# Row-wise infinity norm: sending the bulk store after the last loads, and combining the tail rows one instruction later

## Chip, cores, metric

One core of a Trainium2 chip. The metric is the device time of one execution in microseconds (us), median of several.

## The reference

```python
x = np.random.randn(8192, 8192).astype(np.float32)       # 268 MB
return np.linalg.norm(x, ord=np.inf, axis=1)             # max |x| of each row: 8192 numbers, 32 KB
```

## The kernel before

Everything is read once and reduced on VectorE. 48 rows per partition are "bulk" (24 loads of 8 MB, two rows per partition each). The other 16 rows per partition are "tail": seven tiles in pieces that get smaller, then a last tile of 13 pieces, so that little work is left when the last byte lands. Bulk results go out in one store from the ACT queue, tail results in one from SP at the end. POOL waits for everything and clears the semaphores.

```python
    def absmax(o, i):
        nc.vector.reduce_max(out=o, in_=i, axis=X, apply_absolute_value=True)

    for a in range(A):                      # A = 6
        for n in range(G):                  # G = 4
            t = sbuf.tile([P, W + PAD], F32, tag="t")        # 3 buffers
            nc.sync.dma_start(out=t[:, :W], in_=x_b[a, n])
            absmax(r_bulk[:, a, n * B : (n + 1) * B], t[:, :W].rearrange(...))
    nc.scalar.dma_start(out=out_b, in_=r_bulk[:])            # 768 runs of 32 bytes

    for i, loads in enumerate(TAIL):        # 21 loads, 28 reductions into `part`
        ...
    # last tile
    for j, (b, w) in enumerate(LAST):       # 13 pieces, 2176 down to 640 columns
        final = left[b] == 0
        ...
        nc.sync.dma_start(out=t[:, to : to + w], in_=...)
        if final:
            absmax(r_tail[:, r : r + 1], t[:, to : slot[b] + parts_of[b]])
        else:
            absmax(t[:, k : k + 1], t[:, to : to + w])
        if j == 0:
            absmax(r_tail[:, : n_tail - B], part[:])         # combine the other tail rows
    nc.sync.dma_start(out=out_t, in_=r_tail[:])
```

All SP and ACT transfers share eight completion semaphores ("lanes") in rotation. A transfer is not issued before the previous user of its lane has landed.

## Time and profile before

| | kernel before |
|---|---|
| time, median (range) | 628.01 us (627.74 to 628.76), 3 runs; 627.96 over 6 |
| span in the profile | 626.4 us |
| load queue's share of the 16 DMA engines | 99.4% |
| VectorE busy | 552.9 us, 88% |
| bulk store, issue to landing | 59.1 us |
| SP's wait for the bulk store's lane | 24.3 us |

The loads fill the DMA engines from start to end, so the span is the time to read 268 MB plus a short end. Only what makes the loads end sooner, or shortens the path from the last landing to the end, can count. The lines that carry this are in the prediction.

### The profile page before, as it was taken

How to read it: one execution, taken by the hardware profiler on the slowest of the kernel's cores; microseconds unless marked ns; L12 is line 12 of the kernel's file. 1: busy time of each engine (PE TensorE's matmuls, PEld its weight loads, DVE VectorE, ACT ScalarE, POOL GpSimd, SP SyncE). 2: the span in 40 equal slices, each digit the busy share in tenths (PEclk: the TensorE clock that was granted, in tenths of full speed). 3: DMA queues.
4: the chain of work that ended last, by engine and by line, in shares of the span. 5: the costliest groups of instructions: out<-in, count | busy, mean ns of one | idle time of the engine just before them, and what ended most of it. 6: DMA issues, size and time to landing. Idle time of an engine off the chain costs nothing.

```text
span 626.4 us, 204 instructions
## 1 busy us (share of the span) xinstructions
DVE 552.9 (88%) x67; POOL 0.2 (0%) x4
## 2 busy tenths in 40 slices
DVE  0588988889988889888898888988889999999998
POOL 0000000000000000000000000000000000000000
DMA  9999999999999999999999999999999999999997
GB/s 402 469 402 452 418 452 418 448 423 402 469 402 469 402 469 402 469 402 469 402 469 402 465 406 452 418 452 418 452 404 426 438 428 425 439 423 431 426 422 311
DMA packets 9282, 268.49 MB, mean 429 GB/s; under 512 B 1856, under 2 KB 1856, under 8 KB 3392
## 3 DMA queue, kind: packets, MB, share of 16 engines
q1 hardware_dynamic: 8496, 268.45, 99.4%
q10 hardware_dynamic: 784, 0.02, 0.1%
q14 instruction: 2, 0.02, 0.0%
HBM read 268.44 MB, written 0.03 MB: 429 GB/s over the span
## 4 chain that ended last, share of the span: by engine, by line
DMA 63%; DVE 35%; issue 1%; another core or an unknown queue 0%; DVEq 0%
DMA t<-in_x_dram 63%; DVE r_bulk L140 24%; DVE part L140 8%; DVE t L140 3%; DVEq L220 0%; DVE r_tail L140 0%
## 5 line engine op out<-in xcount | busy, mean ns | idle before, releaser
L140 DVE TENSOR_REDUCE r_bulk<-t 128x2 f32<-128x16384 f32 x24 | 413.3, 17220 | 70.0 <-DMA t<-in_x_dram 70.0
L140 DVE TENSOR_REDUCE part<-t 128x1 f32<-128x8192 f32 (+20 forms) x28 | 121.6, 4410 | 0.9 <-DMA t<-in_x_dram 0.8
L140 DVE TENSOR_REDUCE t<-t 128x1 f32<-128x1664 f32 (+8 forms) x11 | 16.5, 1572 | 0.0
L140 DVE TENSOR_REDUCE r_tail<-t 128x1 f32<-128x644 f32 (+1 forms) x2 | 1.5, 814 | 0.0
L137 DVE MEMSET part<- 128x56 f32 x1 | 0.1, 105 | 0.9 <-PEq L209 0.9
L140 DVE TENSOR_REDUCE r_tail<-part 128x14 f32<-128x56 f32 x1 | 0.2, 211 | 0.0
L209 POOL MEMSET const-bfloat16-1.0<- 128x1 bf16 x1 | 0.1, 101 | 0.0
L209 POOL MEMSET const-uint8-127<- 128x1 uint8 x1 | 0.1, 101 | 0.0
L209 POOL MEMSET const-float32-0.0<- 128x1 f32 x1 | 0.1, 98 | 0.2 <-issue 0.2
L209 POOL MEMSET const-float32-1.0<- 128x1 f32 x1 | 0.1, 98 | 0.0
## 6 DMA issues: line engine op xcount, KB each, us to landing
t<-in_x_dram SPq DMA_DIRECT2D x2, 3392.0 KB, 37.3
t<-in_x_dram SPq DMA_DIRECT2D x1, 5376.0 KB, 40.6
t<-in_x_dram SPq DMA_DIRECT2D x1, 4864.0 KB, 32.9
t<-in_x_dram SPq DMA_DIRECT2D x1, 4800.0 KB, 33.0
t<-in_x_dram SPq DMA_DIRECT2D x1, 4672.0 KB, 34.9
t<-in_x_dram SPq DMA_DIRECT2D x3, 1536.0 KB, 28.7
t<-in_x_dram SPq DMA_DIRECT2D x1, 3520.0 KB, 42.9
t<-in_x_dram SPq DMA_DIRECT2D x1, 3328.0 KB, 40.4
```

The costliest lines, as they stand in the source:

```text
L137: nc.vector.memset(part[:], 0.0)
L140: nc.vector.reduce_max(out=o, in_=i, axis=X, apply_absolute_value=True)
L209: nc = _bacc.Bacc("TRN2", target_bir_lowering=False, num_devices=1)
```

## The change

Its intent: keep the small store out of the stream of loads, and let VectorE begin the last tile without waiting for the partials just written. `NoSync` is an order without a semaphore; `Sync` makes the ACT queue wait for VectorE.

```diff
     def absmax(o, i):
-        nc.vector.reduce_max(out=o, in_=i, axis=X, apply_absolute_value=True)
+        return nc.vector.reduce_max(...)
@@ after the bulk
-    nc.scalar.dma_start(out=out_b, in_=r_bulk[:])
@@ before the last tile
+    def after(ins, first, kind):
+        info = mybir.DependencyInfo(kind, mybir.DependencyReason.SCHED_ONLY)
+        tc.add_manual_dep(ins.ins, first.ins.name, info, reason="order")
@@ in the last tile
-            absmax(t[:, k : k + 1], t[:, to : to + w])
+            done = absmax(t[:, k : k + 1], t[:, to : to + w])
         if j == 0:
-            absmax(r_tail[:, : n_tail - B], part[:])
+            ins = absmax(r_tail[:, : n_tail - B], part[:])
+            after(ins, done, mybir.DependencyClass.NoSync)
+        if j == len(LAST) - 4:
+            ins = nc.scalar.dma_start(out=out_b, in_=r_bulk[:])
+            after(ins, done, mybir.DependencyClass.Sync)
```

More of the change, by code (lines that the diff above doesn't have):

```diff
@@ L139, in absmax @@
     def absmax(o, i):
-        nc.vector.reduce_max(out=o, in_=i, axis=X, apply_absolute_value=True)
+        return nc.vector.reduce_max(
+            out=o, in_=i, axis=X, apply_absolute_value=True
+        )
     for a in range(A):
```

## The prediction

> **What bounds the kernel now.** I read the page first, for which resource is full. These are its first line, the packet total, the queues and the two stores among the DMA issues (KB, then us from issue to landing):
>
> ```profile
> span 626.4 us, 204 instructions
> ...
> DMA packets 9282, 268.49 MB, mean 429 GB/s; under 512 B 1856, under 2 KB 1856, under 8 KB 3392
> ...
> q1 hardware_dynamic: 8496, 268.45, 99.4%
> q10 hardware_dynamic: 784, 0.02, 0.1%
> ...
> out_dram<-r_bulk ACTq DMA_DIRECT2D x1, 24.0 KB, 59.1
> out_dram<-r_tail SPq DMA_DIRECT2D x1, 8.0 KB, 1.4
> ```
>
> The load queue keeps the 16 DMA engines 99.4% busy: the kernel is a 268 MB read at 429 GB/s, with little at either end. The bulk store is 784 tiny packets (768 of 32 bytes and 16 for the semaphore) and takes 59.1 us to land, because it goes out in the middle of that read. So the second thing to read was who waited for it. First the load queue's own waits between 500 and 545 us, then the rates in four stretches (us, DVE busy, POOL busy, clock, DMA share, GB/s):
>
> ```profile
> SPq L158 <- DMA out_dram<-r_bulk: 24.3, 1, 24.3
> ```
>
> ```profile
> 41.20:486.40 445.20, 398.24 (x24) 0.00 (x0) 1.00 1.00 432
> 486.40:544.72 58.32, 57.86 (x10) 0.00 (x0) 1.00 1.00 430
> 544.72:578.44 33.72, 33.72 (x9) 0.00 (x0) 1.00 1.01 432
> ```
>
> ```profile
> 519.00:543.30 24.30, 23.84 (x4) 0.00 (x0) 1.00 1.01 435
> ```
>
> SP really stands for 24.3 us, because the store sits in the rotation of eight completion semaphores and a load needs its lane. But in just those 24.3 us the DMA engines run at a share of 1.01 and 435 GB/s: two loads issued before were still draining. The wait is in the queue, not in the data. What the store does show is the second line: 430 GB/s while its packets are in the stream, against 432 before and after.
>
> Third, the end: the chain of waits, last pieces (start, us, what), and the order of time around 606 us:
>
> ```profile
> 588.91 0.02 issue
> 588.93 17.66 DVE part L140 x7
> 606.59 0.02 issue
> 606.61 0.21 DVE r_tail L140
> 606.82 16.01 DVE t L140 x11
> ```
>
> ```profile
> 604.17 2.41 DVE L140 TENSOR_REDUCE part<-t 128x1 f32<-128x2176 f32 x1
> 606.48 2.76 SPq L179 DMA_DIRECT2D t<-in_x_dram  x2
> 606.61 0.21 DVE L140 TENSOR_REDUCE r_tail<-part 128x14 f32<-128x56 f32 x1
> 606.74 2.41 DVE L140 TENSOR_REDUCE t<-t 128x1 f32<-128x2176 f32 x1
> ```
>
> From 599.1 us VectorE never idles. The first piece of the last tile has landed at 606.46 (SP, which waits for that same semaphore, goes on at 606.48), yet its reduction starts at 606.74. By the trace's semaphore records the pieces land 0.16 to 0.38 us before their reductions start, all the way to the last one (landed 623.61, started 623.86). So the end is set by VectorE running just behind the loads: a fixed amount taken off VectorE after 599.1, or all loads landing earlier, shows in full; either can only move until the other holds it.
>
> **What the Trainium skill says.** "DMA: Bandwidth & Descriptors", section "Queues, rings and completion order", says each DMA engine goes round its queues by packet. The trace agrees: 784/16 = 49 store packets per engine were let in one or two at a time between load packets, first at 487.84, last at 542.95 us. Its section "Issuing engines are not separate DMA queues" says that ACT and SP share the 16 engines; so the store takes time from the loads wherever it overlaps them, as the dip to 430 GB/s shows. "VectorE: DVE Perf Modes", section "The DRAIN you can't avoid", says an instruction that reads what the one just before wrote needs a semaphore, and that one instruction between them removes the hazard. The trace agrees on the cost side: VectorE reductions otherwise start some 80 ns before their predecessor's recorded end (604.168 + 2.410 = 606.578 would allow 606.50), but the one that reads the partials, written just before, started at 606.613, 35 ns after that end. "Perfetto Trace Analysis", section "DMA Instruction — HWDGE (DVE, Sync)", says a write's semaphore follows only after the write is confirmed, slow above all to HBM. The tail store agrees: issued at 624.705, packets from 625.546 to 625.749, landed at 626.131.
>
> **The change part by part.** (1) The store leaves the stream of loads. Each of its 784 packets takes 9 ns in the DMA records: 784 x 9 / 16 = 0.44 us per engine. A second way: the six loads that land between 486.40 and 544.72 bring 49,152 columns, 1.1865 ns each; the bulk loads run at 19.33 us / 16,384 = 1.180. 49,152 x 0.0065 = 0.32 us. I take 0.35 us by which every later load lands earlier. VectorE can follow: the two gaps where it waited for a load (0.46 us before 536.40, 0.36 us before 584.17) mean that it had finished early there and starts with the data.
> (2) SP's 24.3 us wait goes, and the store leaves the lane rotation; the loads behind it are queued about 24 us earlier. Nothing drains faster: 0.
> (3) The reduction of the partials moves behind the first piece of the last tile. It no longer reads what was just written, so piece one can start at 606.50 instead of 606.74, the partials' reduction runs after it, and the second piece starts at 606.50 + 2.326 + 0.128 = 608.95 instead of 609.07: 0.117 us saved (2.326 and 0.128 are the distances from start to start before). The built program shows one new instruction: piece one now has two waits, so a separate semaphore wait stands before it (21 ns where the trace has such). It may not get in until the load has landed at 606.46, so I count 0.08 us. The loads allow it: the smallest lead of a landing over its reduction is 0.16 us.
> (4) The store now goes out when VectorE has finished the tenth of 13 pieces, before at 621.277 + 1.076 = 622.35, in the changed kernel about 621.9. From issue to first packet on a free queue: 0.84 us (tail store) to 1.0 us (first load at 0). So its packets start near 622.8, as the last load data end (623.26 less 0.35 to 0.43). An estimate of its transfer: 49 packets per engine, at some 20 ns each, seen as the distance between two store packets, is 1.0 us; receipt 0.38 us as for the tail store (626.13 - 625.75). Landed near 624.2 us, against about 625.7 for the tail store, which ends the kernel: hidden, 1.5 us to spare.
> (5) The end of the path, tail store 1.43 us and POOL's final wait and clear 0.27 us, stays.
> Sum: 0.35 + 0.08 = 0.43 us off the span, 626.4 to about 626.0; 628.01 to about 627.6 in the times.
>
> **The rivals.**
> *The removed 24.3 us wait is worth microseconds.* For it: it is the longest single wait of the load queue. Against it: the DMA share of 1.01 inside it, and 429 GB/s over the whole span. Even if the whole dip from 432 to 430 were due to it, 58.32 x 2/432 is 0.27 us, and that is counted already. With it true: 625 or less.
> *The late store becomes what ends the kernel.* For it: in the trace the ACT queue took 3.6 us from issue (484.243) to its first packet (487.84). If that belongs to the queue and not to the loads ahead of it, packets start at 625.5, run 1 us and land at 626.9, about 1.2 us after the tail store would have: 628.8. The 32-byte writes to HBM might also need more than 20 ns each; at 60 ns the store would land at 626.1. Against it: 1.0 us on SP's own queue when it was fresh and nothing else ran. I give it one in ten.
> *The store's packets push the last loads.* One DMA engine trails the others by 0.35 us in the last landings (the 16 increments of the last load spread over 1.1 us, the second slowest at 0.74). Store packets that reach it first interleave with its last load packets; a handful at 20 ns is about 0.1 us on the last load: 627.7.
> *The trailing engine itself changes.* Its lag appears at the landing of 584.15 (spread 0.55 us before, 1.06 after), just after an 8 KB instruction packet at 582.08. If that refill falls elsewhere in the changed kernel, the loads' end moves by up to 0.5 us either way: 627.1 or 628.1. This is the largest uncertainty.
>
> **Range and chances.** The centre is 628.01 - 0.43, taken a little lower, 627.5, as 0.44 us is as well founded as 0.35 for part 1. Downwards: refill gone and all packets counted, near 627; upwards: gain eaten by the store or the refill, near 628.2. The three times of the kernel before alone spread over 1.0 us. So 626.8 to 628.3. Two per cent are 12.6 us, which no rival reaches: faster 0.005, within 0.99, slower 0.005.
>
> **What would show it.** Part 1: the stretch between 486 and 545 us at the rate of its neighbours, landings near 606 us about 0.35 us earlier. Part 2: no wait for the bulk store on SP's list, DMA share around 520 to 543 us unchanged. Part 3: the first piece ahead of the partials, starting with no gap, and VectorE some 0.1 us closer to the landings. Part 4: the bulk store's time to landing down from 59.1 to 2 to 3 us, ahead of the tail store's. I am wrong if the bulk store lands after the tail store, if the load rate in the stretch stays at 430, or if the last load lands no earlier than 623.3 us.

## The result

627.63 us (627.56 to 627.77, 6 runs) against 627.96 us (627.74 to 628.76, 6 runs). The ratio is 0.9993, 95% interval 0.998 to 1.0006: within 2%, and the interval holds 1.

The page of the changed kernel, the lines that answer to those in the prediction:

```profile
span 625.7 us, 205 instructions
...
q1 hardware_dynamic: 8496, 268.45, 99.5%
q10 hardware_dynamic: 784, 0.02, 0.1%
...
out_dram<-r_bulk ACTq DMA_DIRECT2D x1, 24.0 KB, 2.0
out_dram<-r_tail SPq DMA_DIRECT2D x1, 8.0 KB, 1.4
```

The same 784 packets now land in 2.0 us instead of 59.1. The load queue's waits (us in total, times, longest) no longer name the store; the time went to other names. Before:

```profile
SPq L158 <- DVE part L140: 35.5, 3, 15.0
SPq L158 <- DMA t<-in_x_dram: 27.0, 9, 5.8
SPq L158 <- DMA out_dram<-r_bulk: 24.3, 1, 24.3
```

and after:

```profile
SPq L159 <- DVE part L140: 47.7, 4, 15.0
SPq L159 <- DMA t<-in_x_dram: 38.9, 11, 6.9
```

The sums are 86.8 us before and 86.6 us after. SP waits as long as it did, only for other things. Next, the order of time around the partials, and at the end:

```profile
603.21 2.41 DVE L140 TENSOR_REDUCE part<-t 128x1 f32<-128x2176 f32 x1
605.52 2.77 SPq L184 DMA_DIRECT2D t<-in_x_dram  x2
605.60 2.42 DVE L140 TENSOR_REDUCE t<-t 128x1 f32<-128x2176 f32 x1
607.94 0.20 DVE L140 TENSOR_REDUCE r_tail<-part 128x14 f32<-128x56 f32 x1
608.05 2.28 DVE L140 TENSOR_REDUCE t<-t 128x1 f32<-128x2048 f32 x1
```

```profile
621.73 0.41 ACTq L200 DMA_DIRECT2D out_dram<-r_bulk  x1
622.48 1.55 DVE L140 TENSOR_REDUCE r_tail<-t 128x1 f32<-128x644 f32 x2
624.05 0.35 SPq L202 DMA_DIRECT2D out_dram<-r_tail  x1
```

The first piece starts 0.08 us after SP saw it land (0.26 us before the change), and the partials' reduction starts 81 ns before its predecessor's end (607.936 against 605.598 + 2.419). At the end the bulk store is 2.3 us ahead of the tail store.

**Where 0.66 us of span went.** The trace's semaphore records give each load's landing (its sixteenth increment). I took four loads as marks: A, landed at 486.40 us before, 1.4 us ahead of the store's first packet; B, at 578.44, after they are over; C, at 608.89, in the last tile; D, the last.

| us | before | after | difference |
|---|---|---|---|
| start to A | 486.396 | 486.112 | 0.284 |
| A to B: the old place of the store | 92.046 | 91.908 | 0.138 |
| B to D | 45.169 | 44.997 | 0.172 |
| landing of D to the last reduction's start | 0.251 | 0.189 | 0.062 |
| from there to the end | 2.535 | 2.528 | 0.007 |
| span | 626.397 | 625.734 | 0.663 |

Of this the store's old place shows 0.14 us and VectorE's order 0.06 us. The first row lies before anything differs between the two programs' loads, so it should be chance. The third was unexplained and is what the experiments had to find. It has two parts of opposite sign (both are in the table below): from B to C the changed kernel is 0.53 us shorter, from C to D 0.36 us longer. The longer part shows in the order of time as a wait of VectorE that was not there before:

```profile
612.35 1.89 DVE L140 TENSOR_REDUCE t<-t 128x1 f32<-128x1664 f32 x1 [0.23 <-DMA t<-in_x_dram]
```

### The profile page after: what moved, and what is told of

It reads as the page before. It is cut to its first block, busy times and chain, and to the rows that moved or that the text cites. A ratio compares the mean times of both kernels' runs of the same rounds, so it can differ in the third digit from the quotient of the medians.

```text
span 625.7 us, 205 instructions
## 1 busy us (share of the span) xinstructions
DVE 552.9 (88%) x67; POOL 0.2 (0%) x4
## 4 chain that ended last, share of the span: by engine, by line
DMA 67%; DVE 31%; issue 1%; another core or an unknown queue 0%; DVEq 0%; SPq 0%
DMA t<-in_x_dram 67%; DVE r_bulk L140 24%; DVE part L140 6%; DVE t L140 2%; DVEq L230 0%; DVE r_tail L140 0%; SPq L159 0%
```

## The experiments

Theory: a store in the stream costs the loads a little, nothing else does, and VectorE's order gives less than 0.1 us. Rivals: SP's removed wait is the gain; VectorE's order is the gain; the difference is chance (when the first loads happen to land, and where two instruction packets fall: 8 KB transfers on the queue that the page lists as q14, kind `instruction`, which may hold up a DMA engine). Eleven kernels ran on three chips, each with five rounds (e4 has four times on record); all results were correct.

| run | change | time | before, same chip | ratio (95%) | A | A to B | B to C | C to D | instruction packets at |
|---|---|---|---|---|---|---|---|---|---|
| (first profile) | kernel before | | | | 486.40 | 92.05 | 30.45 | 14.72 | 582.1, 593.1 |
| (first profile) | the change | | | | 486.11 | 91.91 | 29.92 | 15.07 | 591.9, 610.0 |
| c1_before_again | none | 627.89 | 627.73 | 1.0003 (0.999 to 1.0015) | 486.30 | 92.07 | 30.52 | 14.71 | 582.1, 593.1 |
| e1_store_only | store late | 627.92 | 627.73 | 1.0003 (0.9991 to 1.0016) | 486.54 | 91.93 | 30.17 | 14.71 | 582.5, 592.9 |
| e2_order_only | order | 627.68 | 627.73 | 1.0002 (0.9989 to 1.0015) | 486.32 | 92.06 | 29.93 | 14.74 | 592.8, 609.8 |
| e3_pool_store | early store from GpSimd | 627.88 | 627.73 | 1.0002 (0.9988 to 1.0016) | 486.22 | 92.04 | 30.19 | 14.71 | 582.3, 592.5 |
| c2_after_again | the change again | 627.56 | 627.90 | 0.9996 (0.9982 to 1.0009) | 486.11 | 91.92 | 29.94 | 15.01 | 592.0, 609.5 |
| e4_six_stores | five more stores, ACT | 641.31 | 627.90 | 1.0213 (1.0199 to 1.0227) | | | | | 590.2, 605.7 |
| e5_last_store | store last of all | 628.34 | 627.90 | 1.0007 (0.9994 to 1.0019) | 486.25 | 91.92 | 29.92 | 14.82 | 592.0, 609.9 |
| e6_pad16 | 16 memsets first | 627.93 | 627.90 | 0.9999 (0.9987 to 1.0012) | 486.21 | 92.50 | 29.91 | 14.70 | 490.3, 592.5 |
| e7_six_pool | five more stores, GpSimd | 628.63 | 627.89 | 1.0015 (1.0002 to 1.0027) | 486.83 | 92.22 | 29.87 | 14.71 | 577.6, 592.9 |
| e8_rows192 | store in 192-byte runs | 628.25 | 627.89 | 1.0006 (0.9993 to 1.0018) | 486.40 | 92.01 | 30.25 | 14.72 | 582.5, 592.9 |
| e9_after_pad16 | the change, 16 memsets | 627.66 | 627.89 | 0.9998 (0.9984 to 1.0011) | 486.28 | 92.07 | 29.92 | 14.71 | 490.0, 592.5 |

c1 to e3 shared one chip, c2 to e6 a second, e7 to e9 a third; each group has its own runs of the kernel before.

**c1_before_again**: the kernel before, unchanged.

> Control: the kernel before, unchanged, against itself. Ratio 1.000 within 0.001 by every theory. The profile tells what is chance: in the two profiles so far the loads land 0.28 us earlier in the changed kernel already at 486 us, before the store is issued in either. If that is chance, this control's landing of the load that came at 486.40 us may differ by up to 0.3 us from it. And the 8 KB instruction packet that made one DMA engine trail from 584 us on (spread of the last increments 0.55 to 1.06 us): if its place belongs to the program it comes at about 582 us again; if it is chance it moves.

It came out 0.16 us above its own twin on the same chip, so times here resolve no difference of that size. The kernel before landed A at 486.40 and 486.30; with every kernel whose bulk phase is unchanged the range is 486.11 to 486.54. The 0.28 us in the first row of the sum is within that range: no change made it. The packets came at 582.1 and 593.1 again: their places belong to the program.

**e1_store_only**: the store late, the partials' reduction as before.

```diff
-            ins = absmax(r_tail[:, : n_tail - B], part[:])
-            after(ins, done, mybir.DependencyClass.NoSync)
+            absmax(r_tail[:, : n_tail - B], part[:])
```

> Only the store is moved behind the last loads; the partials' reduction stays ahead of the first piece. Packet theory (the store's packets cost the loads 0.15 to 0.35 us, the reorder is worth 0.1 us or less): span 0.15 to 0.35 us under the kernel before, ratio about 0.9995, no more than 0.1 us slower than the full change. Rival, the gain is VectorE's order: ratio 1.000. On SP's list no wait for the bulk store.

A miss in the time (0.19 us above, where 0.15 to 0.35 below was expected; c1 was 0.16 above with no change at all). In the trace A to B is 91.93 us, as in the full change, and the last load landed at 623.34 us against 623.61: the store's share is there and too small for the clock.

**e2_order_only**: the order alone, the store early.

```diff
-        if j == len(LAST) - 4:
-            ins = nc.scalar.dma_start(out=out_b, in_=r_bulk[:])
-            after(ins, done, mybir.DependencyClass.Sync)
@@ after the bulk
+    nc.scalar.dma_start(out=out_b, in_=r_bulk[:])
```

> Only the partials' reduction is moved behind the first piece; the store stays in the stream of loads. Packet theory: at most 0.12 us (0.0002) faster, and nothing if a load landing late starts VectorE's last chain after it, as in the profile of the changed kernel (at 612.33 us). Order rival: the whole 0.33 us, ratio 0.9995. In the trace the partials' reduction should start 0.08 us before its predecessor's end, not 0.035 us after.

Time: no difference. In the trace A to B is 92.06 us, so the store still costs; the lag of the last reduction behind D is 0.20 us instead of 0.25; the partials' reduction again starts 80 ns before its predecessor's end. And the instruction packets stand at 593 and 610, as in the full change: the order alone moves the one of 582 to 610.

**e3_pool_store**: the old place, another queue.

```diff
-    nc.scalar.dma_start(out=out_b, in_=r_bulk[:])
+    nc.gpsimd.dma_start(out=out_b, in_=r_bulk[:])
```

> The store stays early but goes out from the GpSimd queue, whose semaphore is not in the loads' rotation: the packets stay in the stream, SP's wait of 24.3 us goes. Packet theory: same as the kernel before, ratio 1.000, load rate between 486 and 545 us as before. Rival, the removed wait is the gain: ratio 0.9995 or less, like the full change. SP's list must show no wait for the bulk store, else the run tells nothing.

SP's list names no store, and A to B stays at 92.04:

```profile
SPq L158 <- DVE part L140: 47.5, 4, 15.0
SPq L158 <- DMA t<-in_x_dram: 39.2, 11, 7.0
```

So the 24.3 us wait was worth nothing where it stood, and the transfer itself costs the loads 0.12 us here. One thing was not as planned: this queue wrote the same runs in 32 packets instead of 784 and landed in 7.1 us. So the run took away the wait and most of the packets at once, and the loads gained nothing. The cost is then not that of 49 packets per engine.

**c2_after_again**: the change, unchanged, on another chip.

> Control: the changed kernel again, on another chip. Ratio 0.9990 to 1.0002. In the trace, from the landing of the load that came at 486.40 us to that of the one at 578.44 us: 91.92 us as in both profiles without an early store (92.05 in all four with it). If the place of the 8 KB instruction packets belongs to VectorE's program: 592 and 610 us, not 582 and 593.

As expected in every number: 0.34 us under the kernel before (0.33 the first time), A to B 91.92, packets at 592 and 609.5.

**e4_six_stores**: a store of zeros after each of the first five groups of bulk loads, to the same output; the real one overwrites them.

```diff
+    zero = outp.tile([P, A, G * B], F32)
+    nc.vector.memset(zero[:], 0.0)
@@ at the end of each group a of four bulk loads; done is its last reduction
+        if a < A - 1:
+            ins = nc.scalar.dma_start(out=out_b, in_=zero[:])
+            after(ins, done, mybir.DependencyClass.Sync)
```

> The kernel before with five more stores of the same shape (zeros, to the same output, overwritten by the real store at the end of the bulk), one after each of the first five groups of four bulk loads: five times 784 more packets in the stream of loads. If a store costs the loads 0.13 us, as the distance between landings says (92.05 against 91.92): 0.65 us slower, ratio 1.0010. If it costs the 0.35 to 0.44 us of the prediction: 1.75 to 2.2 us slower, ratio 1.003. If nothing: 1.000. SP may also wait for a lane of one of these stores; each lands within the 77 us between two of them.

13.4 us slower (2.1%, with an interval on both sides of 2%): not one of the sizes expected. The load queue's waits, and two stretches (us, DVE busy, POOL busy, clock, DMA share, GB/s):

```profile
SPq L153 <- DMA out_dram<-zero: 155.2, 4, 40.7
...
SPq L169 <- DMA out_dram<-r_bulk: 31.1, 1, 31.1
SPq L169 <- DMA out_dram<-zero: 31.0, 1, 31.0
```

```profile
275.00:293.30 18.30, 16.16 (x2) 0.00 (x0) 1.00 0.93 402
293.30:300.00 6.70, 6.70 (x1) 0.00 (x0) 1.00 1.02 411
```

Here the lane wait did cost. In the bulk only three buffers are in play. While SP stood for a store from 252.6 to 293.3 us, both loads ahead drained; the last landed at 293.13 and the next, issued at 293.3 into an empty queue, at 315.28, 22.15 us later instead of 19.36: 2.8 us lost. The same happened at 373 and 454 us, and once in the tail (15.8 us for a load of 10,752 columns that took 12.7). Four times 2.8 to 3.0 us are most of the 13.4. The length of a wait alone does not cost: the first one, 33.2 us from 175.1 us, lost nothing (19.37 us to the landing that followed it), since a load was still in the queue at its end and landed 7 us later. So the wait that the prediction called worthless is so only where enough loads stand in the queue.

**e5_last_store**: both stores at once, at the end.

```diff
-        if j == len(LAST) - 4:
+        if j == len(LAST) - 1:
             ins = nc.scalar.dma_start(out=out_b, in_=r_bulk[:])
-            after(ins, done, mybir.DependencyClass.Sync)
+            after(ins, last, mybir.DependencyClass.Sync)      # last: the final reduction
```

> The changed kernel with the bulk store held until the last reduction, so that both stores are issued together at about 624.1 us. In the profile of the change the bulk store took 2.0 us to land, the tail store 1.4: so the end should come 0.5 to 0.7 us later than in the changed kernel, ratio to the kernel before 1.0000 to 1.0008. If the prediction's worst case held (3.6 us from issue to first packet on that queue) it would be 3 us later, ratio 1.004.

Span 626.4 against 625.7, time 0.78 us over the changed kernel on the same chip: slightly over the expected 0.5 to 0.7. The stores' times to landing:

```profile
out_dram<-r_bulk ACTq DMA_DIRECT2D x1, 24.0 KB, 2.1
out_dram<-r_tail SPq DMA_DIRECT2D x1, 8.0 KB, 1.4
```

The tail store's packets went first (624.80 to 625.02 us) and it landed in 1.43 us, as before. The bulk store's ran from 624.96 to 625.48 us, and it landed last, at 626.01, where the changed kernel's last store landed at 625.47. That is 0.54 us of the 0.68 between the spans. The other 0.14 lie behind that landing, where POOL has 0.40 us to go instead of 0.27, with two more waits on its list. That eats the whole gain, so where the late store is placed matters.

**e6_pad16**: the kernel before with a longer VectorE program.

```diff
+    pad = outp.tile([P, 16], F32)
+    for k in range(16):
+        nc.vector.memset(pad[:, k : k + 1], 0.0)
```

> The kernel before with 16 tiny memsets at the start of VectorE's program, 1 to 2 us that lie beside the first load. Ratio 1.000. If the instruction packet at 582 us is VectorE's program crossing a block boundary, it moves 16 VectorE instructions earlier, to somewhere between 490 and 510 us, and the trailing engine's jump with it; if it belongs to another engine or to chance it stays at 582.

The packet of 582 moved to 490.3, the other stayed at 592.5. It is VectorE's program, and the second is not. The jump in the landings moved with it: A to B is 92.50 instead of 92.05, while B to C fell from 30.45 to 29.91. A load counts as landed with the last of its 16 increments; the ninth of them kept its distance from A to B (92.04 us, against 92.06 in the kernel before). So one 8 KB packet delayed one or a few engines, and with them all later landings, by about 0.45 us.

**e7_six_pool**: the six stores again from GpSimd, `nc.gpsimd` in both places of the diff of e4.

> The six stores of the last batch again (five of zeros, then the real one), but from the GpSimd queue, whose semaphore is not in the loads' rotation. If the 13.4 us of that run were SP's waits for the stores' lanes with only two or three loads queued: at most 1 us slower than the kernel before here, and SP's list shows no wait for a store. If they were the stores' own traffic: again some 13 us. If each store costs the loads 0.13 us: the loads end 0.65 us later than before, ratio 1.001; the distance between landings from 41 to 486 us grows by 0.65 us.

No wait for a store, and 0.74 us slower instead of 13.4. A came at 486.83, against a mean of 486.28 in the eleven profiles without a store in the bulk phase: 0.55 us for five stores, 0.11 us each. This agrees with 0.13 us from A to B by another way. Of the kernel's 0.74 us about 0.19 us lie at the end, where POOL has more semaphores to wait for and clear (2.72 us from the last reduction's start to the end, against 2.53). And these stores, too, went out in 32 packets each: that the traffic of 784 packets was not what cost 13.4 us in e4 rests on e4's own trace.

**e8_rows192**: 128 runs of 192 bytes; the loads' addresses change too.

```diff
-    x_b = x[:split].rearrange("(a p n b) c -> a n p (b c)", ...)
-    out_b = out[:split].rearrange("(a p n b) -> p a (n b)", ...)
+    x_b = x[:split].rearrange("(p a n b) c -> a n p (b c)", ...)
+    out_b = out[:split].rearrange("(p a n b) -> p a (n b)", ...)
```

> The kernel before with its bulk rows laid out so that each partition owns 48 consecutive rows: the store is 128 runs of 192 bytes instead of 768 of 32, at the old place in the stream; the loads read other addresses in pieces of the same size. Packet theory: a store of 8 packets per engine costs the loads a sixth of 0.13 us, 486 to 578 us in 91.94 instead of 92.05 us; it lands within about 15 us, so SP's wait of 24.3 us is gone too. Times 0.1 us under the kernel before, not to be told from it. If the loads' new addresses are slower, the bulk loads show it (19.35 us between landings before).

The bulk loads are no slower (A at 486.40, as before). The store landed in 12.9 us and SP did not wait for it, but A to B is 92.01, not 91.94: two thirds of the cost stay with a fifth of the packets (144). With e3 this says that most of the 0.13 us belongs to a store in the stream as such, not to the number of its packets. What makes it up I cannot say. What the number of packets does set is how long the store stays in the stream: 49, 9 and 2 packets per engine took 55.1, 9.0 and 2.4 us from first to last (the kernel before, this one, e3), about 1.1 us each, and with that how long a lane is held.

**e9_after_pad16**: the same 16 memsets in the changed kernel.

> The changed kernel with 16 tiny memsets at the start of VectorE's program. VectorE's instruction packet should move from 610 us to about 490, as it moved from 582 to 490 in the kernel before. If the late place of the packet is part of the gain (it cost the last loads 0.04 to 0.36 us at 610, 0.24 to 0.60 at 582, 0.46 at 490): 0.1 to 0.3 us slower than the changed kernel, span 625.8 to 626.0. If the place does not matter: span 625.7.

The packet moved from 610 to 490.0, and the span stayed at 625.7. It cost only about 0.15 us here (A to B 92.07 against 91.92), where the same place cost 0.45 in e6. So a later place is not in itself cheaper. From the profiles, by excess over 91.92, 92.05, 29.92 or 14.71 us: at 582, 0.25 to 0.60 (five profiles); at 610, 0.03 to 0.36 (four); at 490, 0.45 and 0.15. A likely reading, not shown (the records kept do not tell the engines apart), is that it depends on whether the engine hit is the one that trails.

## Why the prediction was right, point by point

**The time.** 627.5 was forecast with 626.8 to 628.3; measured 627.63, and 627.56 on a second chip. The size is right, but not all of its terms are. That 0.33 us came out where 0.43 was summed is in part luck: the terms that the runs show make 0.19 us, and the rest is no term of the sum: chance in when the loads land, and instruction packets. Two of the prediction's own signs do not tell its cause from others. The last load did land before 623.3 us (623.02), but so it did with the store still early (623.05 in e2, 623.16 in e3), and not with the store late alone (623.34 in e1). And the rate cannot show a cost of 0.13 us: over A to B the view gives 431 GB/s with the store (e3) and without it (the change, e1), so the dip from 432 to 430 was no measure of the store.

**Part 1, the store's packets (0.35 us): the mis-sized term.** It measured 0.13 us: 91.91 to 91.93 us from A to B in four profiles with a late store and no extra packet there, against 92.04 to 92.07 in four with an early one. Two ways had led to 0.32 and 0.44, and both were wrong. Adding up 49 records of 9 ns supposes that records exclude each other; but the windows show DMA shares above 1.00, so they overlap. And the second way compared loads of odd sizes with 64 KB bulk pieces; the same six loads without the store took 58.18 us against 58.32, so 0.15 us of the 0.32 was the store's and the rest is there without it.

**Part 2, SP's wait (0): right**, by e3 and e8: the wait was gone in both, and the loads gained 0.00 and 0.04 us from A to B, though both had fewer packets as well. What decides it is the stock of loads in the queue (e4), as the share of 1.01 during the wait had said.

**Part 3, VectorE's order (0.08 us): right in kind and near in size.** The lag behind the last landing fell by 0.06 us (0.25 to 0.19; it is 0.19 to 0.20 in all five profiles with the new order, 0.24 to 0.26 in all eight with the old). The separate wait does cost: landed 605.506, wait over at 605.533, started 605.598, where VectorE itself would have been free at 605.54. That is 0.06 of the 0.117 us.

**Part 4, the late store: right.** Issued at 621.73 (forecast 621.9), first packet at 622.69 (622.8), landed at 623.73 (624.2). Its 49 packets per engine took 0.52 us, 11 ns each, not 20. The tail store landed at 625.47, 1.74 us later (1.5 forecast). The rival that the ACT queue needs 3.6 us fell: 0.96 us with the loads gone.

**The rival of the trailing engine: real.** The prediction left its sign open and did not tie it to the change. The new order does move VectorE's packet: with its program otherwise unchanged, the packet stands at 582 in all five profiles with the old order and at 610 in all four with the new one. A likely reason, argued and not shown, is the new separate wait before the first piece: VectorE's sequencer cannot pass it before that piece lands at 605.5, and the packet follows some 4 us later, as the other packet, which seems to be SP's, follows SP's issue at 587.97 by 3.95 us. It fits that with the packet moved far ahead of that wait both orders have it at the same place (490.3 in e6, 490.0 in e9). Whether the move gains anything stays open: between the first two profiles 0.17 us, in e9 the span is the same with it elsewhere.

**What adds up.** 0.13 + 0.06 = 0.19 us are shown for the two parts. The 0.33 us between medians is that, plus a share from the instruction packets' places and from chance in when the first loads land, which these runs cannot separate; its interval holds zero. No run beat the changed kernel.

## What to carry to other kernels

In a DMA-bound kernel ask of every wait on the load queue how much is still queued ahead of it: 24.3 us cost nothing, with two loads still in the queue when the wait ended, and 40.7 us cost 2.8 us, where the queue had run empty. A small store in the stream costs little (0.13 us here), but one that shares the loads' semaphores may stop them; give it a queue with its own, or send it when the loads are over and ahead of the last store. Before explaining a tenth of a per cent, run the old kernel against itself: here that alone gave 0.16 us.

## What the Trainium skill lacked or had wrong

- "Runtime: NRT & Kernel Launch", section "Instruction fetch mechanics", calls the cost of crossing a block of instructions mostly hidden. Here two 8 KB instruction packets of 0.3 us each fell among the loads, and VectorE's came with a delay of all later landings by 0.03 to 0.60 us. That the new order of VectorE's instructions moves its place by 28 us (582 to 610) is on no page.
- "DMA: Bandwidth & Descriptors", section "Issuing engine by pattern", calls the sync and scalar path generally faster. Beside a full stream of loads the GpSimd store of the same 24 KB landed in 7.1 us with 32 packets, the ACT store in 59.1 us with 784.
- No page has it that transfers which share rotating completion semaphores can hold each other up: five slow stores on the loads' lanes made the kernel 13.4 us slower, the same stores on another queue, in fewer packets, 0.74 us.
